# Hybrid decoder trunk, one core: the recurrent layer's sum x and its product with the input gate formed on VectorE instead of GpSimd, three small state copies moved the other way, and all state rows in one tile with one load and one store

## The chip, the cores and the metric

The kernel runs on one core of a Trainium2 chip. Times are device microseconds (us) of one execution of the whole program; several executions give a median. A separate execution is recorded by the hardware profiler. Its span is counted from its first to its last recorded instruction, and its own time is a little longer than the span. In the rows of the profile PE is TensorE's matmuls, PEld its weight loads, DVE is VectorE, ACT is ScalarE, POOL is GpSimd and SP is SyncE, which here only issues DMAs.

## What is computed

The reference runs two layers over 1024 prompt positions and 8 further one-token sequences, in float32. Layer 0 mixes tokens with a gated linear recurrence, layer 1 with sliding-window attention; a squared-ReLU MLP follows each. The change touches layer 0's mixer alone:

```python
def recurrent_block(x, h0, conv_prev, w_in, conv_w, conv_b, w_a, b_a, w_x, b_x, lam, w_out):
    u = x @ w_in
    gate, xr = jnp.split(u, 2, axis=-1)
    xc, conv_new = causal_conv(xr, conv_prev, conv_w, conv_b)
    y, h_new = rg_lru(xc, h0, w_a, b_a, w_x, b_x, lam)
    return (y * jax.nn.gelu(gate)) @ w_out, h_new, conv_new
```

`rg_lru` forms two gates r and i as sigmoids of small products of xc, a decay a = exp(-8 r softplus(-lam)), an input u = sqrt(1 - a²) (i xc), and scans h = a h + u along the positions. Besides its output the layer returns the new states: the last h of the prompt and of each of the 8 sequences, and the last three inputs of the convolution for each of them.

## The kernel before

Features lie on partitions and the 1032 tokens on the free axis, so the width of 1024 is eight tiles of 128x1032, m = 0 to 7; a matmul takes a third of the tokens (344). Full precision comes from splitting each operand in a high and a low part, `hi` (a cast on ACT, lines 165 and 253) and `lo` (a subtraction on DVE, lines 166 and 254), and from three matmuls per product (line 226).

Layer 0's mixer is a list of stages, `LRU` (line 55): c1 c0 x4 g0 c2 c3 r0 c4 x5 g1 c5 r1 x7 x6 g2 r2 c7 o5 c6 o0 o1 o3 g3 r3 o6 o2 o4 o7, after `xr_first`, which computes x for m = 0 to 3. The stages are these:

- x (`xr_stage`, `conv_evac`): the projection; DVE takes each third out of PSUM (line 1129, at high priority) and POOL starts the convolution from it (line 1130).
- c (`conv`): three taps on DVE for the prompt (line 1135), two small copies that keep the last columns, into `cst` (line 1136) and `cvp` (line 1137), three small operations for the 8 sequences that read `cst` (line 1139), then the split into `xch` and `xcl`.
- g (`gates`): for a pair of tiles (2 kb, 2 kb + 1) four products, whose PSUM banks ACT empties with sigmoids at high priority (line 1163). The results are `ri`.
- r (`recur`): for each tile of the pair t = xch + xcl on POOL (line 1172) and i = i t on POOL (line 1173). Then ACT overwrites t with a tanh (line 1175), so it waits for line 1173; then exp (line 1177) and squares (line 1182) on ACT, line 1183 on DVE, a square root on ACT (line 1185), and on DVE the product (line 1188), the scan (line 1189), two operations of 8 columns for the sequences (lines 1190 and 1191) and a copy of the last states into `hno` (line 1192).
- o (`gate_out`): the gate's projection, emptied by DVE (line 1201), GeLU on ACT (line 1202), the product with t in place on DVE (line 1203), and the split for the layer's last product.

Each engine has one queue and takes its instructions in order. That order isn't the order of the program text: a scheduler fills the queues by its own estimate of when each instruction is ready, by priority, where earlier text means higher priority. A wait at the head of a queue therefore holds all behind it. Tiles of 128x1032 come from a pool of 33 (`A`) and one of 12 (`W`); a stage starts only when a slot is free. Weights are fetched by SP (line 159) into a few raw buffers, ahead of their split. One split of a weight in the recurrent layer, that of unit 13, is done by POOL (line 166) and not by DVE.

The states lie in four tiles: `cst` (the old three inputs of each sequence and the new one), `h0`, `cvp` and `hno`. `cst` and `h0` are loaded by two DMAs on SP (lines 1093 and 1095); three DMAs on SP store the new states after stage r3 (lines 1213 to 1215).

Of the kernel before, what the change touches and what calls it, by code (L numbers as in the profile page):

```python
# [10 lines left out]
F32 = mybir.dt.float32  # L11
F32R = mybir.dt.float32r
AF = mybir.ActivationFunctionType
ALU = mybir.AluOpType
PSUM = bass.MemoryType.PSUM

P = 128
D = 1024
M8 = D // P
SEQ = 1024  # L20
NS = 8
T = SEQ + NS
CH = T // 3
NCH = 3
DFF = 4096
NB = SEQ // P
HALF = T // 2
CHUNKS = [range(0, 3), range(3, 6), range(6, 9), range(9, 12), range(12, 14)]
NSP = CHUNKS[-1][-1] + 1
RQ = 2 * P * max(len(c) for c in CHUNKS)  # L30
QT = T // 4
NPAIR = DFF // (2 * P)
# [27 lines left out]
def trunk(ctx: ExitStack, tc: tile.TileContext, I, O):  # L60
    nc = tc.nc
    pe, act, dve, pool, sp = nc.tensor, nc.scalar, nc.vector, nc.gpsimd, nc.sync

    cp = ctx.enter_context(tc.tile_pool(name="cp", bufs=1))
# [24 lines left out]
    def nm(s):  # L89
        cnt[0] += 1  # L90
        return f"{s}{cnt[0]}"

    def A(s="a"):
        return ap.tile([P, T], F32, tag="A", name=nm(s))

    def W(s="w"):
        return wp.tile([P, T], F32, tag="W", name=nm(s))

    def S(s="s"):
        return small["pool"].tile([P, CH], F32, tag="S", name=nm(s))  # L100

    BANKS = {"N": 1, "P": 3, "S": 2, "T": 1, "O": 1}
    ring = ["P", "P", "P", "S", "S", "T"]
    turn = [0]

    def B(tag=None):
        if tag is None:
            tag = ring[turn[0] % len(ring)]
            turn[0] += 1
        return psum["pool"].tile([P, 512], F32, tag=tag, bufs=BANKS[tag], name=nm("b" + tag))  # L110
# [14 lines left out]
    def cs(c):  # L125
        return slice(c * CH, (c + 1) * CH)
# [12 lines left out]
    def V(n, m=0):  # L139
        o, _ = VEC[n]  # L140
        return vec[:, o + m:o + m + 1]
# [34 lines left out]
    for o in [("x", m) for m in range(4)] + LRU:  # L176
        if o[0] == "g":
            units.append(("gate", o[1], I["w_gate"][o[1]], W))
        elif o[0] in "xo":
            m = o[1] + (8 if o[0] == "x" else 0)  # L180
# [71 lines left out]
    def split_act_dve(hi, lo, src, sl, eng=dve):  # L252
        act.copy(r_(hi[:, sl]), src)
        eng.tensor_tensor(r_(lo[:, sl]), src, hi[:, sl], ALU.subtract)
# [437 lines left out]
    def attention(hs):  # L692
# [9 lines left out]
        qrow = aux[:, 0:P]  # L702
        qblk = qrow.rearrange("p (n t u i) -> p n t u i", n=NS, t=2, u=2)
        pool.memset(qrow, 0.0)
        ks = aux[:, P:P + 2 * NS].rearrange("p (t n) -> p t n", t=2)
        den = [cp.tile([P, 4], F32, name=f"den{i}") for i in range(4)]
# [82 lines left out]
        def v_proj():  # L789
# [22 lines left out]
            ps = B("T")  # L812
            mms(ps[:NS, :256], slice(SEQ, T))
            vo = S("vo")
            act.copy(vo[:NS, :256], ps[:NS, :256])
            sp.dma_start(vnew.rearrange("h (n j) -> (h n) j", n=4), vo[:NS, :256])

# [271 lines left out]
            ensure(3)  # L1089

    sp.dma_start(con, I["con"])
    cst = cp.tile([P, M8, 4, NS], F32, name="cst")
    sp.dma_start(cst[:, :, 0:3, :], I["conv_state"])
    h0 = cp.tile([P, M8, NS], F32, name="h0")
    sp.dma_start(h0, I["h_state"])
    cvp = cp.tile([P, M8, 3], F32, name="cvp")
    hno = cp.tile([P, M8, 1 + NS], F32, name="hno")


    sp8 = cp.tile([P, M8], F32, name="sp8")  # L1100
    lam = nsp8 = VV("lam")
# [18 lines left out]
    ys = {}  # L1120
# [11 lines left out]
    def conv(m):  # L1132
        xr, xc = xrc.pop(m)
        for d, w in ((1, "cw2"), (2, "cw1"), (3, "cw0")):
            dve.scalar_tensor_tensor(xc[:, d:SEQ], xr[:, 0:SEQ - d], V(w, m), xc[:, d:SEQ], ALU.mult, ALU.add)  # L1135
        dve.tensor_copy(cst[:, m, 3, :], xr[:, SEQ:T])
        dve.tensor_copy(cvp[:, m, :], xr[:, SEQ - 3:SEQ])
        for k, w in ((2, "cw2"), (1, "cw1"), (0, "cw0")):
            dve.scalar_tensor_tensor(xc[:, SEQ:T], cst[:, m, k, :], V(w, m), xc[:, SEQ:T], ALU.mult, ALU.add)
        hi, lo = A("xch"), A("xcl")  # L1140
        split_act_dve(hi, lo, xc, slice(0, T))
        xcs[m] = (hi, lo)
# [23 lines left out]
    def recur(kb):  # L1166
        ms = (2 * kb, 2 * kb + 1)
        for m in ms:
            i = rr[m, 1]
            xh, xl = xcs.pop(m)  # L1170
            ys[m] = (W if m in (2, 3, 5, 7) else A)("t")
            pool.tensor_tensor(ys[m], xh, xl, ALU.add)  # L1172
            pool.tensor_tensor(i, i, ys[m], ALU.mult)  # L1173
        for m in ms:
            act.activation(ys[m], rr[m, 0], AF.Tanh, scale=sp8[:, m:m + 1])
        for m in ms:
            act.activation(rr[m, 0], rr[m, 0], AF.Exp, scale=nsp8[:, m:m + 1])
        for m in ms:
            r, t = rr[m, 0], ys[m]
            for c in range(NCH):  # L1180
                a2 = S("a2")
                act.activation(a2, r[:, cs(c)], AF.Square)
                dve.scalar_tensor_tensor(t[:, cs(c)], a2, 1.0, t[:, cs(c)], ALU.add, ALU.mult)
        for m in ms:
            act.activation(ys[m], ys[m], AF.Sqrt)
        for m in ms:
            r, i, t = rr.pop((m, 0)), rr.pop((m, 1)), ys[m]
            dve.tensor_tensor(i, t, i, ALU.mult)
            dve.tensor_tensor_scan(t[:, :SEQ], r[:, :SEQ], i[:, :SEQ], 0.0, ALU.mult, ALU.add)
            dve.tensor_tensor(t[:, SEQ:T], r[:, SEQ:T], h0[:, m, :], ALU.mult)  # L1190
            dve.tensor_tensor(t[:, SEQ:T], t[:, SEQ:T], i[:, SEQ:T], ALU.add)
            dve.tensor_copy(hno[:, m, :], t[:, SEQ - 1:T])

    gos = {}

# [14 lines left out]
    for what, i in LRU:  # L1210
        stages[what](i)
        if (what, i) == ("r", 3):
            sp.dma_start(O["conv"][:, :, 3:27].rearrange("p m (k n) -> p m k n", k=3), cst[:, :, 1:4, :])
            sp.dma_start(O["conv"][:, :, 0:3], cvp)
            sp.dma_start(O["h"], hno)
    gl = [gos[m] for m in range(M8)]
    pin_tables()
    spill, spill0, spill1 = [tc.dram_tile([M8, P, T], F32, name=f"spill{i}") for i in range(3)]
# [31 lines left out]

_OUT_SHAPES = {
    "y": (M8, P, T),
    "conv": (P, M8, 27),
    "h": (P, M8, 9),
    "k": (2, P, P),
    "v": (P, 256),
    "ks": (2, P, D),
# [41 lines left out]
def _layout(a):  # L1299
    f = lambda n: np.asarray(a[n])  # L1300
    out = {}
    x = np.concatenate([f("x_prompt")[0], f("x_sample")[:, 0]], 0)
    out["xT"] = x.T.reshape(M8, P, T)
    out["w_in"] = _mtiles(f("lru_w_in")[0])
    out["w_gate"] = np.stack([f("lru_w_a")[0], f("lru_w_x")[0]], 1).reshape(4, 2, 2, P, 256).transpose(0, 3, 2, 1, 4).reshape(4, P, D)
    out["w_out0"] = _mtiles(f("lru_w_out")[0])
    out["w_up"] = np.stack([_pair_blocks(f("mlp_w_up")[l]) for l in range(2)])
    out["w_dn"] = np.stack([_down_units(f("mlp_w_down")[l]) for l in range(2)])
    perm = np.concatenate([np.arange(h * 64, h * 64 + 64) for h in HEAD_PERM])
    wqkv = f("attn_w_qkv")[0]  # L1310
    wv = wqkv[:, 1280:1536].reshape(2, 4, P, 256).transpose(0, 2, 1, 3).reshape(2, P, D)
    out["w_qkv"] = np.concatenate([_mtiles(wqkv[:, perm]), _mtiles(wqkv[:, 1024:1280]), wv])
    out["w_out1"] = _mtiles(f("attn_w_out")[0][perm])
    vec = np.zeros((P, NVEC), np.float32)

    def put(n, v):
        o, w = VEC[n]
        vec[:, o:o + w] = v

    cols = lambda v: v.reshape(M8, P).T  # L1320
    put("g_mix0", cols(f("norm_mix_g")[0]))
    put("g_mix1", cols(f("norm_mix_g")[1]))
    put("g_mlp0", cols(f("norm_mlp_g")[0]))
    put("g_mlp1", cols(f("norm_mlp_g")[1]))
    for k in range(4):
        put(f"cw{k}", cols(f("lru_conv_w")[0, k]))
    put("cb", cols(f("lru_conv_b")[0]))
    put("ba", cols(f("lru_b_a")[0]))
    put("bx", cols(f("lru_b_x")[0]))
    put("lam", cols(f("lru_lambda")[0]))  # L1330
    put("qg", np.tile(f("attn_q_norm")[0], 2)[:, None])
    put("kg", np.tile(f("attn_k_norm")[0], 2)[:, None])
    sinks = f("attn_sinks")[0]
    put("sinks", np.broadcast_to(sinks, (P, 16)))
    heads = np.array([(2 * p + u) * 4 + i for n in range(NS) for p in range(2) for u in range(2) for i in range(4)])
    put("sink_row", sinks[heads][:, None])
    put("slope_row", np.array([-SLOPES[h] for h in heads], np.float32)[:, None])
    put("eps", np.float32(EPS))
    out["vec"] = vec
    out["con"], out["dist_s"] = _constants()  # L1340
    out["conv_state"] = f("state_rglru_conv")[0].reshape(NS, 3, M8, P).transpose(3, 2, 1, 0)
    out["h_state"] = f("state_rglru_h")[0].reshape(NS, M8, P).transpose(2, 1, 0)
    kc = f("cache_swa_k")[0][:, 1:]
    out["k_cache"] = kc.reshape(NS, 127, 2, P).transpose(2, 3, 0, 1)
    out["v_cache"] = f("cache_swa_v")[0][:, 1:].reshape(NS, 127, 256).transpose(1, 0, 2)
    return {k: np.ascontiguousarray(v) for k, v in out.items()}
# [34 lines left out]
```

## Time and profile before

| what | us |
|---|---|
| median of 3 executions | 2031.12 (2030.24 to 2034.45) |
| profiled execution, its own time | 2033.93 |
| its span | 2032.2 |
| busy in the span: PE, DVE, ACT, POOL | 2001.2, 1413.9, 1056.3, 352.8 |

The recurrent layer takes the first 260 us or so of the span, and its list of stages begins at about 50 us. Attention and the two MLPs take the rest. Of the views used below, the windows give the busy time of each engine in stretches of the span with the granted TensorE clock (PEclk, where 1.00 is full speed); the waits give for each engine what it sat idle for; the timeline gives the instructions in order, neighbours of one kind merged, as start, duration, engine, line, operation, output and inputs.

### The profile page before, as it was taken

What the parts mean: (1) busy time and instruction counts of PE and PEld (TensorE: products, weight loads), DVE (VectorE), ACT (ScalarE), POOL (GpSimd) and SP (SyncE); (2) the same over time, 40 slices, a digit from 0 to 9 for tenths busy, and PEclk for the clock granted to TensorE, in tenths of its full rate; (3) what the DMA queues carried; (4) which work ended last, traced back from release to release, by engine and by line L of the source; (5) the groups of instructions that cost most, each with busy time, mean ns of one, the idle gap of its engine ahead of it and who ended that gap; (6) DMA issues with size and microseconds to landing.
All of it is one profiled execution on the core that took longest, in us unless ns stands there. A gap on an engine that the chain in (4) does not pass through costs nothing.

```text
span 2032.2 us, 38742 instructions
## 1 busy us (share of the span) xinstructions
PE 2001.2 (98%) x15106; PEld 1956.2 (96%) x15106; DVE 1413.9 (70%) x2673; ACT 1056.3 (52%) x2090; POOL 352.8 (17%) x562
## 2 busy tenths in 40 slices
PE   8989999999999999999999999999999999999999
PEld 8979999999999999999988887899999999999999
DVE  7887637876766867666846677569776767766663
ACT  6475635543343655555457777546434346555550
POOL 2541100000000333321003444100000003332220
PEclk9989999999999999999999999999999999999999
DMA  5102142244344787877443435712534446887783
GB/s 176 52 32 55 53 164 87 99 152 152 136 152 162 245 231 206 229 197 178 130 109 84 107 94 168 247 59 70 189 138 150 142 166 226 228 217 212 203 199 105
DMA packets 121047, 304.87 MB, mean 150 GB/s; under 512 B 20888, under 2 KB 53152, under 8 KB 120864
## 3 DMA queue, kind: packets, MB, share of 16 engines
q1 hardware_dynamic: 64864, 135.41, 22.1%
q0 software_dynamic: 28352, 98.30, 19.0%
q10 hardware_dynamic: 27648, 68.70, 9.2%
q8 instruction: 118, 1.93, 0.4%
q14 instruction: 65, 0.53, 0.1%
HBM read 176.22 MB, written 113.44 MB: 143 GB/s over the span
## 4 chain that ended last, share of the span: by engine, by line
PE 89%; DVE 2%; ACT 2%; issue 1%; POOL 1%; DMA 1%; SPq 0%; ACTq 0%; POOLq 0%
PE bD L529 60%; PE bP L226 11%; PE bS L226 6%; PE bP L771 4%; PE bT L226 3%; PE bO L892 1%; PE bS L851 1%; PE bT L871 1%; PE bN L717 1%; POOL t L1172 1%; PE bS L799 1%; POOL ri L1173 0%; DVE wl L166 0%; DVE xc L1135 0%; DMA od0l<-o 0%
## 5 line engine op out<-in xcount | busy, mean ns | idle before, releaser
L529 PE MATMUL bD<-op,op 128*128 128x258 f32 x5376 | 648.5, 283 | 0.0
L529 PEld LDWEIGHTS bD<-op,op 128*128 128x128 f32 x5376 | 647.9, 190 | 0.4
L529 PE MATMUL bD<-tl,op 128*128 128x258 f32 x4704 | 567.7, 283 | 0.0
L529 PEld LDWEIGHTS bD<-tl,op 128*128 128x128 f32 x4704 | 566.7, 190 | 0.8 <-DVE ho L640 0.2
L542 POOL DMA_DIRECT2D tl<-hsum x196 | 116.1, 712 | 913.1 <-DMA hsum<-he 420.8
L396 DVE TENSOR_TENSOR op<-ws,op 128x512 fp32r<-128x512 f32 (+2 forms) x288 | 170.6, 598 | 80.0 <-ACT op L395 80.0
L402 DVE TENSOR_TENSOR tl<-tl 128x516 fp32r<-128x516 f32 x196 | 130.9, 694 | 122.7 <-ACT tl L401 122.6
L636 ACT COPY ho<-bD 128x516 f32<-128x516 f32 x144 | 85.1, 591 | 244.1 <-PE bD L529 241.7
L395 ACT CAST op<-ws 128x512 fp32r<-128x512 f32 (+2 forms) x288 | 155.8, 550 | 56.2 <-DVE op L396 27.1
L396 DVE TENSOR_TENSOR op<-raw,op 128x512 fp32r<-128x512 f32 (+2 forms) x216 | 124.5, 597 | 57.8 <-ACT op L395 57.8
L636 ACT COPY he<-bD 128x516 f32<-128x516 f32 x144 | 84.0, 583 | 134.6 <-PE bD L529 125.3
L395 ACT CAST op<-raw 128x512 fp32r<-128x512 f32 (+2 forms) x216 | 114.5, 549 | 34.9 <-PE bD L529 22.7
L401 ACT CAST tl<-tl 128x516 fp32r<-128x516 f32 x196 | 114.9, 627 | 2.8 <-DMA tl<-hsum 2.8
L649 ACT ACTIVATE ho<-ho 128x1032 f32<-128x1032 f32 x32 | 34.2, 1070 | 107.3 <-DVE ho L648 107.3
L166 DVE TENSOR_TENSOR wl<-raw,wh 128x1024 fp32r<-128x1024 f32 (+1 forms) x57 | 68.2, 1202 | 25.5 <-ACT wh L165 20.6
L862 POOL TENSOR_SCALAR se<-se,den 128x256 f32<-128x256 f32 (+1 forms) x128 | 66.1, 521 | 77.2 <-DVE den L860 75.3
L165 ACT CAST wh<-raw 128x1024 fp32r<-128x1024 f32 (+1 forms) x60 | 58.6, 988 | 37.7 <-DMA raw<-w_in 15.9
L855 DVE CUSTOM_DVE_ANT_0 se<-bS,bias,nsink 128x256 f32<-128x256 f32 (+1 forms) x128 | 56.4, 461 | 21.6 <-PE bS L851 16.8
L655 POOL DMA_DIRECT2D spill<-ho x32 | 28.7, 896 | 242.2 <-DVE ho L644 232.6
L858 ACT ACTIVATE se<-se,den 128x257 f32<-128x257 f32 (+1 forms) x128 | 63.0, 496 | 14.7 <-DVE den L855 13.0
L644 DVE TENSOR_TENSOR ho<-bD,ho 128x516 f32<-128x516 f32 x72 | 49.8, 692 | 23.0 <-PE bD L529 23.0
L640 DVE TENSOR_TENSOR ho<-bD,ho 128x516 f32<-128x516 f32 x72 | 49.7, 690 | 16.0 <-PE bD L529 9.1
(299 smaller groups left out, 3745.5 us busy)
## 6 DMA issues: line engine op xcount, KB each, us to landing
tl<-hsum POOLq DMA_DIRECT2D x196, 258.0 KB, 7.8
raw<-w_up SPq DMA_DIRECT2D x64, 512.0 KB, 3.7
raw<-w_dn SPq DMA_DIRECT2D x64, 384.0 KB, 5.6
spill<-ho POOLq DMA_DIRECT2D x32, 516.0 KB, 6.7
spill<-he POOLq DMA_DIRECT2D x32, 516.0 KB, 7.9
hsum<-ho ACTq DMA_DIRECT2D x28, 516.0 KB, 3.7
hsum<-he ACTq DMA_DIRECT2D x28, 516.0 KB, 2.7
hsum<-ts ACTq DMA_DIRECT2D x28, 516.0 KB, 3.4
```

The costliest lines, as they stand in the source:

```text
L166: eng.tensor_tensor(r_(lo[:, sl]), raw[:, sl], hi[:, sl], ALU.subtract)
L226: pe.matmul(o, lhsT=r_(wt[:, col(k):col(k) + P]), rhs=r_(xt[:, cs(c)]), start=(k == first and a == 0), stop=(k == final and a == 2))
L395: act.copy(r_(t[:, 0:n]), src)
L396: dve.tensor_tensor(r_(t[:, n:2 * n]), src, t[:, 0:n], ALU.subtract)
L401: act.copy(r_(hi), lo)
L402: dve.tensor_tensor(r_(lo), lo, hi, ALU.subtract)
L529: pe.matmul(d[:, 512 * b:512 * b + QT], lhsT=r_(wt[:, j * P:j * P + P]), rhs=r_(xt[:, QT * b:QT * b + QT]), start=first and j == 0 and a = ...
L542: pool.dma_start(t[:, n:2 * n], src)
L636: last["copy"] = act.copy(t, f).ins
L771: pe.matmul(ps[c], lhsT=r_(wt[:, k * P:k * P + P]), rhs=r_(xt[:, cs(c)]), start=(k == 0 and a == 0), stop=(k == M8 - 1 and a == 2))
L858: act.activation(se[:, u, 256 - n:257], se[:, u, 256 - n:257], AF.Exp, scale=-1.0, bias=dn[:, u:u + 1], accum_out=dn[:, 2 + u:3 + u])
L862: pool.tensor_scalar(e, e, dn[:, 2 + u:3 + u], 0.0, ALU.mult, ALU.add)
```

## The change

1. Lines 1172 and 1173, eight instructions each on 128x1032, go from POOL to DVE.
2. The copies of lines 1136, 1137 and 1192, eight each on 128x8, 128x3 and 128x9, go from DVE to POOL.
3. The four state tiles become one, `st`, of 52 columns per m. One DMA loads it, with the host leaving gaps where results will be written, and one DMA stores all of it after stage r3. The host cuts the results out.

```diff
-    cst = cp.tile([P, M8, 4, NS], F32, name="cst")
-    sp.dma_start(cst[:, :, 0:3, :], I["conv_state"])
-    h0 = cp.tile([P, M8, NS], F32, name="h0")
-    sp.dma_start(h0, I["h_state"])
-    cvp = cp.tile([P, M8, 3], F32, name="cvp")
-    hno = cp.tile([P, M8, 1 + NS], F32, name="hno")
-
+    st = cp.tile([P, M8, NST], F32, name="st")
+    sp.dma_start(st, I["states"])
+    h0, hno, cvp = st[:, :, 35:43], st[:, :, 43:52], st[:, :, 32:35]
+
+    def cst(m, k):
+        return st[:, m, k * NS:(k + 1) * NS]
...
-        dve.tensor_copy(cst[:, m, 3, :], xr[:, SEQ:T])
-        dve.tensor_copy(cvp[:, m, :], xr[:, SEQ - 3:SEQ])
+        pool.tensor_copy(cst(m, 3), xr[:, SEQ:T])
+        pool.tensor_copy(cvp[:, m, :], xr[:, SEQ - 3:SEQ])
         for k, w in ((2, "cw2"), (1, "cw1"), (0, "cw0")):
-            dve.scalar_tensor_tensor(xc[:, SEQ:T], cst[:, m, k, :], V(w, m), xc[:, SEQ:T], ALU.mult, ALU.add)
+            dve.scalar_tensor_tensor(xc[:, SEQ:T], cst(m, k), V(w, m), xc[:, SEQ:T], ALU.mult, ALU.add)
...
-            pool.tensor_tensor(ys[m], xh, xl, ALU.add)
-            pool.tensor_tensor(i, i, ys[m], ALU.mult)
+            dve.tensor_tensor(ys[m], xh, xl, ALU.add)
+            dve.tensor_tensor(i, i, ys[m], ALU.mult)
...
-            dve.tensor_copy(hno[:, m, :], t[:, SEQ - 1:T])
+            pool.tensor_copy(hno[:, m, :], t[:, SEQ - 1:T])
...
-            sp.dma_start(O["conv"][:, :, 3:27].rearrange("p m (k n) -> p m k n", k=3), cst[:, :, 1:4, :])
-            sp.dma_start(O["conv"][:, :, 0:3], cvp)
-            sp.dma_start(O["h"], hno)
+            sp.dma_start(O["states"], st)
```

More of the change, by code (lines that the diff above doesn't have):

```diff
@@ L21 @@
 NS = 8
+NST = 52
 T = SEQ + NS
@@ L1252 @@
     "y": (M8, P, T),
-    "conv": (P, M8, 27),
-    "h": (P, M8, 9),
+    "states": (P, M8, NST),
     "k": (2, P, P),
@@ L1340, in _layout @@
     out["con"], out["dist_s"] = _constants()
-    out["conv_state"] = f("state_rglru_conv")[0].reshape(NS, 3, M8, P).transpose(3, 2, 1, 0)
-    out["h_state"] = f("state_rglru_h")[0].reshape(NS, M8, P).transpose(2, 1, 0)
+    conv = f("state_rglru_conv")[0].reshape(NS, 3, M8, P).transpose(3, 2, 1, 0).reshape(P, M8, 24)
+    h = f("state_rglru_h")[0].reshape(NS, M8, P).transpose(2, 1, 0)
+    gap = lambda n: np.zeros((P, M8, n), np.float32)
+    out["states"] = np.concatenate([conv, gap(11), h, gap(9)], 2)
     kc = f("cache_swa_k")[0][:, 1:]
@@ L1369 @@
     ys = y[SEQ:].reshape(NS, 1, D)
-    h = o["h"].transpose(2, 1, 0).reshape(9, D)
+    st = o["states"].transpose(2, 1, 0).reshape(NST, D)
+    h = st[43:]
     hp = h[0].reshape(1, 1, D)
     hsm = h[1:].reshape(1, NS, D)
-    cv = o["conv"].transpose(2, 1, 0).reshape(27, D)
-    cvp = cv[:3].reshape(1, 1, 3, D)
-    cvs = cv[3:].reshape(3, NS, D).transpose(1, 0, 2).reshape(1, NS, 3, D)
+    cvp = st[32:35].reshape(1, 1, 3, D)
+    cvs = st[8:32].reshape(3, NS, D).transpose(1, 0, 2).reshape(1, NS, 3, D)
     kp = o["k"].reshape(256, P).T.reshape(1, 1, P, 4, 64)
```

## The prediction

> **What bounds the kernel now.** I read the page first, for which engine sets the end.
>
> ```profile
> PE 2001.2 (98%) x15106; PEld 1956.2 (96%) x15106; DVE 1413.9 (70%) x2673; ACT 1056.3 (52%) x2090; POOL 352.8 (17%) x562
> ...
> PE 89%; DVE 2%; ACT 2%; issue 1%; POOL 1%; DMA 1%; SPq 0%; ACTq 0%; POOLq 0%
> ```
>
> PE is busy 98% of the span and carries 89% of the chain. The change removes no matmul, so it can win only where PE stands still or runs at a lowered clock inside the recurrent layer. PE's waits in the first 420 us, then windows cut at its gaps (stretch, length, then busy us of PE, PEld, DVE, ACT, POOL with counts, PEclk), show where that is.
>
> ```profile
> PE bP L226 <- ACT ri L1163: 6.3, 3, 5.0
> PE bS L226 <- DVE xr L1129: 3.9, 1, 3.9
> ```
>
> ```profile
> 101.12:106.09 4.97, 0.01 (x2) 0.00 (x1) 3.41 (x7) 4.94 (x10) 4.58 (x4) 0.72 0.00 0
> 106.09:111.20 5.11, 5.07 (x19) 4.49 (x19) 5.11 (x10) 5.05 (x7) 0.00 (x0) 0.61 0.02 3
> 111.20:114.52 3.32, 2.61 (x15) 2.33 (x15) 2.51 (x4) 2.30 (x6) 0.00 (x0) 1.00 0.00 0
> ...
> 140.77:144.62 3.85, 0.00 (x0) 0.00 (x0) 3.85 (x6) 1.14 (x3) 0.00 (x0) 0.95 0.00 0
> 144.62:151.08 6.46, 6.46 (x22) 6.18 (x22) 6.44 (x11) 2.24 (x4) 6.40 (x5) 0.50 0.47 162
> ```
>
> There are two real stalls. **Stall 1**: 4.97 us idle for ACT's sigmoids of g1, then 5.11 us at a clock of 0.61, which costs another 5.11 x 0.39 = 2.0. **Stall 2**: 3.85 us idle for DVE to empty x6's banks, then 6.46 us at 0.50, another 3.2. Together they cost 14.0 us. The third row holds 3.32 - 2.61 = 0.7 us of idle time and keeps 1.00.
>
> **Why PE stalls.** ACT's order behind stall 1, and POOL's:
>
> ```profile
> ACT t L1175 <- POOL ri L1173: 15.1, 5, 6.7
> POOL ri L1173 <- ACT ri L1163: 12.5, 3, 9.4
> ```
>
> ```profile
> 46.20 0.63 POOL L1130 TENSOR_SCALAR xc<-xr,vec 128x344 f32<-128x344 f32 x1 [3.72 <-DVE xr L1129]
> ...
> 82.21 3.37 POOL L1172 TENSOR_TENSOR t<-xch,xcl 128x1032 f32<-128x1032 f32 x1 [4.36 <-ACT ri L1163]
> 88.10 3.34 POOL L1172 TENSOR_TENSOR t<-xch,xcl 128x1032 f32<-128x1032 f32 x1 [2.52 <-DVE xcl L254]
> 91.40 5.78 POOL L1173 TENSOR_TENSOR ri<-ri,t 128x1032 f32<-128x1032 f32 x2
> ...
> 119.72 3.80 POOL L1173 TENSOR_TENSOR ri<-ri,t 128x1032 f32<-128x1032 f32 x1 [2.25 <-ACT ri L1163]
> ...
> 137.59 3.06 POOL L166 TENSOR_TENSOR wl<-raw,wh 128x1024 fp32r<-128x1024 f32 x1 [8.74 <-ACT wh L165]
> ```
>
> ```profile
> 97.22 1.16 ACT L1175 ACTIVATE t<-ri,sp 128x1032 f32<-128x1032 f32 x1 [1.23 <-POOL ri L1173]
> ...
> 105.49 1.43 ACT L1163 ACTIVATE ri<-bP,vec 128x344 f32<-128x344 f32 x3
> ...
> 119.04 0.55 ACT L1163 ACTIVATE ri<-bT,vec 128x344 f32<-128x344 f32 x1
> ```
>
> POOL ends r0's second product at 91.40 + 5.78 = 97.18. The second tanh starts at 97.22, and from there to the sigmoid at 105.49 ACT is busy with r0's exponentials, squares and table loads. So POOL's end sets stall 1, one for one: 8.3 us later the bank comes free, and PE resumes at 106.09.
>
> **The same work on DVE.** Two lines' instructions, durations in ns (min/median/max):
>
> ```profile
> L1188 DVE TENSOR_TENSOR ri<-t,ri x8: 1225/1230/1235, 109.7 to 232.9; 128x1032 f32<-128x1032 f32 x8
> ```
>
> ```profile
> L1136 DVE COPY cst<-xr x8: 157/163/172, 50.3 to 161.4; 128x8 f32<-128x8 f32 x8
> ```
>
> Line 1188 is the same operation on the same shape, so each moved instruction takes 1.23 us instead of the 2.9 (half of 5.78) to 3.8 of the rows above; sixteen add 19.7 us to DVE. What DVE loses is seen in its timeline:
>
> ```profile
> 83.17 2.44 DVE L1139 SCALAR_TENSOR_TENSOR xc<-cst,vec,xc 128x8 f32<-128x8 f32 x1
> 85.53 1.21 DVE L166 TENSOR_TENSOR wl<-raw,wh 128x1024 fp32r<-128x1024 f32 x1
> 86.66 0.22 DVE L1139 SCALAR_TENSOR_TENSOR xc<-cst,vec,xc 128x8 f32<-128x8 f32 x1
> 86.80 5.73 DVE L254 TENSOR_TENSOR xcl<-xc,xch 128x1032 fp32r<-128x1032 f32 x3
> ...
> 119.03 2.29 DVE L1189 TENSOR_TENSOR_SCAN t<-ri,ri 128x1024 f32<-128x1024 f32 x1
> 121.24 2.32 DVE L1190 TENSOR_TENSOR t<-ri,h 128x8 f32<-128x8 f32 x1
> ...
> 138.38 2.29 DVE L1190 TENSOR_TENSOR t<-ri,h 128x8 f32<-128x8 f32 x1
> ...
> 142.85 0.15 DVE L1190 TENSOR_TENSOR t<-ri,h 128x8 f32<-128x8 f32 x1
> 142.93 1.21 DVE L166 TENSOR_TENSOR wl<-raw,wh 128x1024 fp32r<-128x1024 f32 x1
> 144.07 0.93 DVE L1129 TENSOR_TENSOR xr<-bS,rt 128x344 f32<-128x344 f32 x2
> ```
>
> An 8-column operation with two inputs takes 0.15 to 0.22 us, but 2.3 to 2.4 us when POOL's long sum or product runs beside it (83.17 beside 82.21, 121.24 beside 119.72): the two exclude each other. At 138.38 it is POOL's weight split, which stays.
>
> *Stall 1.* DVE's three splits end at 86.80 + 5.73 = 92.53. Without POOL beside them, 83.17 loses 2.2 and the splits lose 5.73 - 3 x 1.23 = 2.0; r0's four moved instructions add 4.9. Even if the last product comes last, it ends at 92.53 - 4.2 + 4.9 = 93.2, instead of 97.18. The copies of c0 to c4 (ten) come before: 0.4 us, below. That makes 93.6, a gain of 3.6: PE would idle 1.4 instead of 4.97.
>
> *Stall 2.* r1's last product starts on POOL when the last sigmoid is there (119.04 + 0.55) and ends at 123.52. On DVE it meets the scan of 119.03: ahead of it the product ends at 120.8, behind it at 122.6; I take the middle, 1.8 earlier than now. The scans behind it, and with them the emptying at 144.07, follow. Idle goes from 3.85 to 2.0. r1's other three instructions cost DVE 3.7; its wait of 2.2 at 121.24 goes, and the rest falls in idle time of 3.98 us before line 1188 at 117.76:
>
> ```profile
> 117.76 1.23 DVE L1188 TENSOR_TENSOR ri<-t,ri 128x1032 f32<-128x1032 f32 x1 [3.98 <-ACT t L1185]
> ```
>
> *The clock.* After 0.7 us of idle it stayed at 1.00, after 3.85 it was 0.50. Idle times of 1.4 and 2.0 lie between; both are nearer to 0.7, so I let the slow stretches go (2.0 and 3.2). If they stay, the sum is 5.4 instead of 10.6.
> The Trainium skill ("TensorE: Matmul & The Clock Gate", section "Why this matters for your kernels") bids one leave no PE gap above about 3 us between bursts, else the clock falls to half. The trace agrees at both ends (0.7 us at 1.00, 3.85 us at 0.50), and by that rule the sum is 10.6.
>
> *The copies on POOL.* The trace has no small copy on POOL. Bounds: 0, and 0.63 us, POOL's 344-column operation at 46.20 alone. The DVE copy of the same shape takes 0.16; I take 0.2, being nearer to it in size, so ten cost DVE at most 10 x 0.04 = 0.4 if each holds DVE up for its whole time.
> Against this change speaks the Trainium skill, "SBUF — State Buffer", section "SBUF: two separate sides": VectorE and GpSimd share a port pair as an exclusive lock, held for a whole instruction. The trace agrees (0.15 against 2.3 us); by it every copy on POOL can stop DVE, at its full length. [...]
>
> *Waits added.* Line 1203 writes over t in place, so its last third waits for POOL's copy into the states; on DVE weight splits and PSUM emptying (lines 166, 1201) queue behind it. At 0.2 us, eight times, I cost it at nothing: PE runs without a gap there, on six banks. Without that cover it is up to 8 x 0.63 = 5.0.
>
> ```profile
> 178.00:203.00 25.00, 25.00 (x161) 25.00 (x160) 18.22 (x32) 9.73 (x14) 1.66 (x1) 1.00 0.27 86
> ```
>
> *DMAs.* The load is read first at 53.5 us, long after its issue:
>
> ```profile
> L1139 DVE SCALAR_TENSOR_TENSOR xc<-cst,vec,xc x24: 211/220/2435, 53.5 to 162.1; 128x8 f32<-128x8 f32 x24
> ...
> L1093 SPq DMA_DIRECT2D cst<-conv_state x1: 654/654/654, 19.9 to 19.9; - x1
> ```
>
> ```profile
> SPq L1215 <- DVE hno L1192: 21.8, 1, 21.8
> SPq L1213 <- DVE xc L1139: 17.1, 1, 17.1
> ```
>
> Of SP's two waits for stores the second stays, now for POOL's last copy, with the w_out loads behind it as today; the first, with w_in loads behind, goes. PE has no wait for weights there, so neither counts. The rows of the one tile are disjoint. Were the tile ordered as a whole, c5's reads would come after r0's last copy, behind 121.24 + 2.32 = 123.6, with some 4 us to its split; PE takes x5 only in g2, which starts 3 us ahead of the gap at 140.77. Hidden by some 10 us.
>
> **Sum.** Stall 1: 3.6 + 2.0; stall 2: 1.8 + 3.2; together 10.6. The profiled execution took 2033.93, so 2023.3 for its like; it lay 2.8 above the median of 2031.12, from which I predict 2020.5.
>
> **Rivals.**
>
> - *Half of it* (2025.7): the clock falls after the shorter gaps too, or stall 2 stays as DVE's order puts the scans ahead of x6's emptying (142.93, then 144.07, as now). 5.4 to 5.6 us. For it: that order comes from estimates made before the run. Against: both chains start earlier.
> - *Given back* (2031.1): a moved product waits for its sigmoid at the head of DVE's queue. POOL waited 12.5 us so in three places, at no cost. On DVE 3.98 us of idle time cover part of the 9.4; the remaining 5.4 stand against the scan and x6's emptying and eat the gain of stall 1 (5.6), while stall 2 stays.
> - *Slower* (2036): the copies on POOL hold DVE up. At x us each the last product of r0 ends at 93.2 + 10 (x - 0.16); from x = 0.56 on stall 1 isn't shorter. At 0.63 it is 0.7 longer, six copies of c5, r0 and r1 lengthen stall 2 by 6 x 0.47 = 2.8, and of the 5.0 us of waits before line 1203 a third, 1.7, comes through to PE, whose six banks cover the rest: 5.2 in all, or 8.5 with all 5.0. For it: DVE is the fuller engine. Against: POOL's time for 8 columns should lie well below that for 344.
> - *Nothing done*: both moves are explicit engine names, so the instructions move; no chance of its own.
>
> **How the numbers follow.** Chances: forecast 0.41, half 0.20, given back 0.17, slower 0.22. A measurement can tell about 0.2% (4 us) from no change: faster 0.61, same 0.17, slower 0.22. Lower end: both stalls with their slow stretches gone (14.0), the small gap as well (0.7), and 0.9 for the spread of the runs below their median (2030.24): 2015.5. Upper end: 2037, with the likelier half of the slower case. Left out are some 0.02 below and 0.1 above. The forecast alone spans 2015.5 to 2024.
>
> **What would show it.** Right: lines 1172 and 1173 on DVE at 1.23 us; no 2.3 us operation of 8 columns in r0 to r2 save beside line 166; the second tanh of r0 about 94, the sigmoid of g1 about 102; PEclk at 1.00 from 76 to 152; POOL's copies near 0.2. Wrong: a PE wait for `xr` or `ri` of over 3 us, a DVE wait for ACT's `ri` of some us before line 1173, or copies of 0.5 us and more. Were PE 10 us early and the total unchanged, the time would have gone to a new wait after 150 us.

## The result and the profile after

The changed kernel takes 2017.72 us, the median of 6 executions (2017.08 to 2019.35), against 2031.48 for the kernel before beside it (6 executions, 2030.24 to 2034.45). The ratio is 0.9932, with a 95% interval of 0.9919 to 0.9944: faster by 0.68%, or 13.8 us. The profiled execution took 2018.72 us, its span is 2016.9; before it was 2033.93 and 2032.2.

The page of the kernel after, its busy times and its chain:

```profile
PE 1995.5 (99%) x15106; PEld 1951.8 (97%) x15106; DVE 1411.6 (70%) x2665; ACT 1054.7 (52%) x2089; POOL 321.9 (16%) x570
...
PE 92%; DVE 4%; ACT 2%; issue 1%; DMA 1%; POOL 0%; SPq 0%; ACTq 0%; DVEq 0%
```

The matmuls are the same 15106. DVE, which took over sixteen instructions of 128x1032, isn't busier than before (1413.9): the 19.7 us of the new work are set off by the copies that left and by the eight-column operations and splits that POOL's long instructions no longer hold up. POOL lost 30.9 us. What the change won must then be time in which PE stood still or ran slowly. Windows over the part of the recurrent layer around both stalls, before and then after (stretch, length, busy us and instructions of PE, PEld, DVE, ACT and POOL, granted clock, DMA share, GB/s):

```profile
76.00:203.00 127.00, 117.42 (x710) 115.58 (x709) 100.96 (x134) 80.02 (x110) 50.24 (x25) 0.95 0.16 43
```

```profile
76.00:203.00 127.00, 125.78 (x793) 124.48 (x792) 105.20 (x138) 88.62 (x126) 20.07 (x26) 1.00 0.15 47
```

In the same 127 us PE now does 793 matmuls instead of 710, at a clock of 1.00 instead of 0.95. A matmul takes 0.155 us at full clock (161 in a stretch of 25.00 us without a gap, in the first row below), so 83 of them are 12.9 us. The two profiled executions differ by 15.2 us, and the medians by 13.8: most of the gain comes from this stretch. The two windows that held the stalls, in the kernel after:

```profile
102.00:127.00 25.00, 25.00 (x161) 25.00 (x161) 22.41 (x32) 24.84 (x35) 3.36 (x7) 1.00 0.04 9
127.00:152.00 25.00, 24.43 (x151) 23.54 (x150) 23.98 (x28) 13.84 (x20) 10.98 (x8) 1.00 0.26 78
```

PE has no gap at all in the first and 0.57 us in the second. The waits of PE in the first 420 us, where before stood 6.3 us for ACT's `ri` (one of 5.0) and 3.9 for DVE's `xr`, say the same; `xr` isn't on the list any more, and the longest wait for `ri` is 0.7 (total, times, longest):

```profile
PE bP L227 <- ACT ri L1163: 1.2, 2, 0.7
```

How stall 1 went: DVE's timeline around r0, and ACT's (start, duration, engine, line, operation, in brackets the idle time before and what ended it).

```profile
88.23 2.37 DVE L1172 TENSOR_TENSOR t<-xch,xcl 128x1032 f32<-128x1032 f32 x2
90.52 2.37 DVE L1173 TENSOR_TENSOR ri<-ri,t 128x1032 f32<-128x1032 f32 x2
```

```profile
91.84 2.24 ACT L1175 ACTIVATE t<-ri,sp 128x1032 f32<-128x1032 f32 x2 [2.38 <-DVE ri L1173]
...
97.51 0.47 ACT L1182 ACTIVATE a<-ri 128x344 f32<-128x344 f32 x1
...
99.29 1.43 ACT L1163 ACTIVATE ri<-bP,vec 128x344 f32<-128x344 f32 x3
```

r0's last product ends at 90.52 + 2.37 = 92.89 instead of 97.18, and g1's first sigmoid starts at 99.29 instead of 105.49: 4.3 us of that is the product, the rest is ACT's order. Only one of r0's six squares (line 1182) stands ahead of the sigmoids; the others follow later.

How stall 2 went: the first of r1's scans on DVE before, and DVE's timeline around both scans after.

```profile
136.18 2.28 DVE L1189 TENSOR_TENSOR_SCAN t<-ri,ri 128x1024 f32<-128x1024 f32 x1
```

```profile
128.43 2.27 DVE L1189 TENSOR_TENSOR_SCAN t<-ri,ri 128x1024 f32<-128x1024 f32 x1
130.63 0.90 DVE L1129 TENSOR_TENSOR xr<-bS,rt 128x344 f32<-128x344 f32 x2
...
131.95 2.27 DVE L1189 TENSOR_TENSOR_SCAN t<-ri,ri 128x1024 f32<-128x1024 f32 x1
```

x6's emptying (line 1129) starts at 130.63, between r1's two scans. Before, it stood behind both scans and a weight split, at 144.07. Of these 13.4 us, 7.8 are those by which the first scan itself starts earlier; the other 5.7 are the order, since DVE's queue now has the emptying behind one scan only.

### The profile page after: what moved, and what is told of

Same layout as the page of the kernel before. It is cut to its first block, busy times and chain, and to the rows that moved or that the text cites. A ratio compares the mean times of both kernels' runs of the same rounds, so it can differ in the third digit from the quotient of the medians.

```text
span 2016.9 us, 38731 instructions
## 1 busy us (share of the span) xinstructions
PE 1995.5 (99%) x15106; PEld 1951.8 (97%) x15106; DVE 1411.6 (70%) x2665; ACT 1054.7 (52%) x2089; POOL 321.9 (16%) x570
## 4 chain that ended last, share of the span: by engine, by line
PE 92%; DVE 4%; ACT 2%; issue 1%; DMA 1%; POOL 0%; SPq 0%; ACTq 0%; DVEq 0%
PE bD L530 60%; PE bP L227 12%; PE bS L227 6%; PE bP L772 4%; PE bT L227 3%; PE bS L852 1%; PE bO L893 1%; PE bT L872 1%; PE bN L718 1%; DVE sq L278 1%; PE bS L800 1%; DVE wl L167 0%; DMA raw<-w_in 0%; ACT wh L166 0%; DVE t L1189 0%
## 5 line engine op out<-in xcount | busy, mean ns | idle before, releaser
L166 ACT CAST wh<-raw 128x1024 fp32r<-128x1024 f32 (+1 forms) x60 | 58.7, 988 | 38.8 <-DMA raw<-w_in 12.9
L645 DVE TENSOR_TENSOR ho<-bD,ho 128x516 f32<-128x516 f32 x72 | 49.7, 690 | 22.9 <-PE bD L530 22.9
L273 ACT ACTIVATE sq<-y 128x344 f32<-128x344 f32 x48 | 23.6, 492 | 71.4 <-DVE y L363 60.8
```

## The theories

Three explanations of the 13.8 us had to be told apart; each expectation below says in its own words what it makes of its run.

- *Length*: POOL's sums and products took 2.4 to 3.8 us each where DVE takes 1.23. r0's last product ended late, and with it ACT's sigmoids; the rest followed from that.
- *Exclusion*: POOL's long instructions held up DVE's, so that it is their presence beside DVE's work that counted, whichever of them moves.
- *States*: the copies on POOL, the one tile and the fewer DMAs bring some of the time.

A further question came up with the trace of after: whether stall 2 went because DVE had less to do, or because the queue's order changed, and what changed it.

## The experiments

Ratios are to the kernel before, run on the same chip, with 95% intervals. The gaps and clocks are those of one profiled execution each; starts differ by about 1 us between executions, so gaps are compared and not absolute times. Line numbers are those of each run's own kernel: the weight split of line 166 is line 167 in the kernel after and all that come from it, and an edit shifts the lines behind it.

### The moves alone: e1_moves_only

The kernel before, with nothing but lines 1172 and 1173 changed.

```diff
-            pool.tensor_tensor(ys[m], xh, xl, ALU.add)
-            pool.tensor_tensor(i, i, ys[m], ALU.mult)
+            dve.tensor_tensor(ys[m], xh, xl, ALU.add)
+            dve.tensor_tensor(i, i, ys[m], ALU.mult)
```

> The kernel before with only lines 1172 and 1173 on VectorE; copies, tiles and DMAs as before. Theory 1 (the early end of the product frees ACT, so PE's banks come free in time) and theory 2 (VectorE is no longer held up by GpSimd's long instructions) both expect all of the gain: 2016 to 2020 us, no PE wait over 1 us in the recurrent layer. Theory 3 (the copies off VectorE, the one tile or SP's missing wait matter) expects at least a third of the 14 us to be missing: 2022 us or more.

Measured: 0.9938 (0.9921 to 0.9954). In the profiled execution both stalls are gone, and x6's emptying stands between r1's scans as in after. That execution was the fastest of four, 2016.45 us; the other three took 2020.90 to 2021.90. So the two moved lines bring the whole gain as far as can be told: a part of 1 or 2 us for the states, the copies on POOL and the DMAs isn't excluded, but they are not the cause of the gain.

### The states alone: e2_states_only

The kernel after, with both lines back on POOL.

```diff
-            dve.tensor_tensor(ys[m], xh, xl, ALU.add)
-            dve.tensor_tensor(i, i, ys[m], ALU.mult)
+            pool.tensor_tensor(ys[m], xh, xl, ALU.add)
+            pool.tensor_tensor(i, i, ys[m], ALU.mult)
```

> The kernel after with the sum and the product back on GpSimd; copies on GpSimd and one tile as after. Theories 1 and 2 expect no gain: 2029 to 2034 us, both PE stalls there. Theory 3 expects 2026 us or less.

Measured: 0.9983 (0.9974 to 0.9992), 3.5 us by the ratio and 2.7 by the medians; 2030.34 us lies where theories 1 and 2 put it. Stall 1 stays, but stall 2 is shorter, which neither expected. PE's waits, and POOL's timeline:

```profile
PE bP L227 <- ACT ri L1163: 6.0, 3, 4.8
...
PE bS L227 <- DVE xr L1129: 2.1, 2, 1.7
```

```profile
140.08 1.13 POOL L1192 COPY st<-t 128x9 f32<-128x9 f32 x1 [11.22 <-DVE t L1190]
141.18 2.37 POOL L167 TENSOR_TENSOR wl<-raw,wh 128x1024 fp32r<-128x1024 f32 x1
```

A copy into the states, moved to POOL, waits there for r1's eight-column operations on DVE (line 1190), and POOL's weight split is queued behind it. The split therefore no longer runs beside r1's scan chain, as it did at 137.59 before, where it held an eight-column operation on DVE for 2.29 us. So the copies do something on their own, by way of POOL's queue; with the moves in place e1_moves_only and after don't show anything of it, stall 2 being gone then.

### The sum alone: e3_sum_only

The kernel after, with the product (line 1173) back on POOL.

```diff
-            dve.tensor_tensor(i, i, ys[m], ALU.mult)
+            pool.tensor_tensor(i, i, ys[m], ALU.mult)
```

> The kernel after with the product (line 1173) back on GpSimd, the sum on VectorE. Theory 1: r0's two products take 2 x 2.4 us on GpSimd after the sums, so the last ends at about 95.4 instead of 97.2 before and 92.9 after; stall 1 keeps some 3 us and stall 2 stays, 2025 to 2030 us. Theory 2: half of the long GpSimd instructions are gone, half of the gain, 2023 to 2026 us.

Measured: 0.9957 (0.994 to 0.9973), 2024.61 us: in the range of theory 2 and just below that of theory 1. Around stall 1 PE has gaps of 1.04, 1.81 and 0.71 us, and the clock stays at 1.00 behind them. At r1 the gaps are 0.88 and 0.42 us, so stall 2 didn't stay, as theory 1 had it, though x6's emptying is behind both scans and the split again. POOL does r0's two products in a row, beside DVE's work:

```profile
88.43 6.64 POOL L1173 TENSOR_TENSOR ri<-ri,t 128x1032 f32<-128x1032 f32 x2 [11.81 <-ACT xch L254]
```

```profile
89.35 3.45 DVE L255 TENSOR_TENSOR xcl<-xc,xch 128x1032 fp32r<-128x1032 f32 x1
92.72 4.58 DVE L1172 TENSOR_TENSOR t<-xch,xcl 128x1032 f32<-128x1032 f32 x2
```

The products end at 95.07, between the 92.89 of after and the 97.18 of before (by more than the 1 us of the starts), and the gaps lie between as well. That is the order that the length of the chain through r0 would give, but length isn't alone here: a split takes 3.45 us instead of 1.23 and two sums 4.58 instead of 2.37. The gap of 1.04 is a wait for DVE, which empties x5's banks only behind them, at 97.23.

### The product alone: e4_product_only

The kernel after, with the sum (line 1172) back on POOL.

```diff
-            dve.tensor_tensor(ys[m], xh, xl, ALU.add)
+            pool.tensor_tensor(ys[m], xh, xl, ALU.add)
```

> The kernel after with the sum (line 1172) back on GpSimd, the product on VectorE. Theory 1: the sums are ready before the last sigmoid but for r0's second one, so only the product's length counts; r0's last product ends at about 92 to 94, nearly all of the gain, 2017 to 2021 us. Theory 2: half of the long GpSimd instructions are gone, half of the gain, 2023 to 2026 us.

Measured: 0.9994 (0.9985 to 1.0004), no gain that can be told from none; neither expectation had that. At stall 1 the gaps are 1.30 and 2.34 us; behind the second the clock fell. Stall 2 became longer than before. PE's longest wait and the rows of DVE and POOL ahead of it:

```profile
PE bS L227 <- DVE xr L1129: 6.7, 2, 5.4
```

```profile
129.68 4.57 DVE L1188 TENSOR_TENSOR ri<-t,ri 128x1032 f32<-128x1032 f32 x2
134.18 4.52 DVE L1189 TENSOR_TENSOR_SCAN t<-ri,ri 128x1024 f32<-128x1024 f32 x1
```

```profile
130.36 2.80 POOL L167 TENSOR_TENSOR wl<-raw,wh 128x1024 fp32r<-128x1024 f32 x1 [1.75 <-ACT wh L166]
...
134.14 2.41 POOL L1172 TENSOR_TENSOR t<-xch,xcl 128x1032 f32<-128x1032 f32 x1 [0.98 <-PE bT L227]
```

The two products of line 1188 take 4.57 us beside POOL's split, against 2.36 in after, and the scan takes 4.52 beside POOL's sum, against 2.27. x6's emptying stands behind both scans again, at 142.21. So one moved line wins nothing when the other meets DVE's chain at a worse place: exclusion is real, but it is priced by where the two meet.

### After again, for the same chip: e5_after_again

The kernel after unchanged, as the base for the runs beside it.

> The kernel after once more, as the measure for the three runs beside it on this chip: 0.9932 of the kernel before, as first measured, within 0.1%.

Measured: 0.9936 (0.9923 to 0.995), median 2018.71 us, with the same gaps.

### Only r0 back on POOL: e6_r0_pool

The kernel after, with the sum and the product of r0, four instructions of sixteen, on POOL.

```diff
-            dve.tensor_tensor(ys[m], xh, xl, ALU.add)
-            dve.tensor_tensor(i, i, ys[m], ALU.mult)
+            (pool if kb == 0 else dve).tensor_tensor(ys[m], xh, xl, ALU.add)
+            (pool if kb == 0 else dve).tensor_tensor(i, i, ys[m], ALU.mult)
```

> The kernel after with the sum and the product of r0 alone back on GpSimd; r1 to r3 on VectorE. New theory (two stalls with two causes: the late product in r0 makes stall 1; GpSimd's long instructions beside r1's scans, and the place of x6's emptying in VectorE's queue, make stall 2): stall 1 comes back with its slow clock, 7 us, stall 2 at most in part; 2024 to 2027 us. Rival (r0's delay alone makes both): both stalls, 2029 us or more.

Measured: 0.9987 (0.9978 to 0.9996). The four instructions take back most of the gain. POOL's products, then DVE's queue at stall 2:

```profile
89.77 6.78 POOL L1173 TENSOR_TENSOR ri<-ri,t 128x1032 f32<-128x1032 f32 x2
```

```profile
134.49 2.28 DVE L1189 TENSOR_TENSOR_SCAN t<-ri,ri 128x1024 f32<-128x1024 f32 x1
...
136.75 2.28 DVE L1189 TENSOR_TENSOR_SCAN t<-ri,ri 128x1024 f32<-128x1024 f32 x1
...
139.08 1.21 DVE L167 TENSOR_TENSOR wl<-raw,wh 128x1024 fp32r<-128x1024 f32 x1
140.22 0.50 DVE L1129 TENSOR_TENSOR xr<-bS,rt 128x344 f32<-128x344 f32 x1
```

r0's last product ends at 96.55 (the profile starts about 1 us earlier than that of before), PE idles 1.14 and 3.71 us and then runs at a lowered clock: stall 1 is back. r1 has both operations on DVE as in after, and yet x6's emptying is behind both scans and the split again. The gaps there are 1.04 and 0.42 us, at a clock of 1.00. So neither expectation holds whole: 2030.46 us is the rival's time, but stall 2 is back only in small part. What four instructions of r0 decide is stall 1 and, with nothing changed at r1, the order of DVE's queue there; e9_squares_first shows by what way.

### x6's emptying behind the scans: e7_empty_behind

The kernel after with one thing more, an order within DVE's own queue, which needs no semaphore (`NoSync`): x6's emptying comes after r1's second scan. No work is added. `last` only keeps an instruction by name, here the later scan of each pair.

```diff
-            dve.tensor_tensor(xr[:, cs(c)], o, rx[:, cs(c)], ALU.mult)
+            e = dve.tensor_tensor(xr[:, cs(c)], o, rx[:, cs(c)], ALU.mult)
+            if m == 6:
+                tc.add_manual_dep(e.ins, last['scan', 1].name, mybir.DependencyInfo(mybir.DependencyClass.NoSync, mybir.DependencyReason.DATA), reason='order')
...
-            dve.tensor_tensor_scan(t[:, :SEQ], r[:, :SEQ], i[:, :SEQ], 0.0, ALU.mult, ALU.add)
+            last['scan', kb] = dve.tensor_tensor_scan(t[:, :SEQ], r[:, :SEQ], i[:, :SEQ], 0.0, ALU.mult, ALU.add).ins
```

> The kernel after with an edge that only orders VectorE's queue: x6's emptying (line 1129) goes behind r1's second scan instead of between the two. Nothing is computed differently. If the queue's order at this place matters: the emptying starts 2.3 us later, at 132.9, PE idles 1.7 us, and the time rises by 1.7 us if the clock holds, by 3 to 5 if it falls. Rival (the order is of no weight, only the early products count): no PE wait there, no change.

Measured: 0.995 (0.9938 to 0.9963), median 2022.43, 3.7 us more than the kernel after beside it. The two intervals overlap; that a gap opened is seen in the trace. PE's timeline, and a window from the gap on:

```profile
132.16 0.85 PE L227 MATMUL bS<-xch,wh 128*128 128x344 f32 x2 [1.60 <-DVE xr L1129]
```

```profile
131.00:136.00 5.00, 3.84 (x15) 3.37 (x16) 4.91 (x10) 1.64 (x3) 3.69 (x3) 0.79 0.17 26
```

One scan of 2.28 us ahead of the emptying opens a gap of 1.60 us, and the clock falls behind it. From 76 to 203 us PE does 778 matmuls, and in the run of after beside it 792:

```profile
76.00:203.00 127.00, 124.74 (x778) 123.57 (x777) 103.00 (x136) 88.52 (x126) 16.70 (x25) 0.99 0.16 46
```

14 x 0.155 = 2.2 us are lost there, by the medians 3.7. So the place of three short instructions in one queue costs some 2 to 4 us of the 13.8, and part of that is the clock, which other runs below show to hold behind gaps as long.

### The squares ahead of the sigmoids: e9_squares_first

The kernel after, with g1's first three sigmoids ordered behind all six squares of r0 in ACT's queue.

```diff
-                        act.activation(o[:, cs(c)], ps[c], AF.Sigmoid, bias=V(b, 2 * kb + mm))
+                        e = act.activation(o[:, cs(c)], ps[c], AF.Sigmoid, bias=V(b, 2 * kb + mm))
+                        if (kb, mm, g) == (1, 0, 0):
+                            tc.add_manual_dep(e.ins, last['sqr', 0].name, mybir.DependencyInfo(mybir.DependencyClass.NoSync, mybir.DependencyReason.DATA), reason='order')
...
-                act.activation(a2, r[:, cs(c)], AF.Square)
+                last['sqr', kb] = act.activation(a2, r[:, cs(c)], AF.Square).ins
```

> The kernel after with an edge that only orders ScalarE's queue: g1's first three sigmoids go behind all six squares of r0, as in the kernel before, instead of behind the first square. If the early product alone removes stall 1: the sigmoid starts about 101.2 instead of 99.3, PE idles about 1 us at most, and the time rises by 0 to 1.5 us. If the new order of ScalarE's queue does the work: 4 us or more.

Measured: 0.9941 (0.9928 to 0.9953), 1.5 us more than after in the medians, which the intervals don't resolve. ACT's and PE's timelines:

```profile
96.53 2.37 ACT L1184 ACTIVATE a<-ri 128x344 f32<-128x344 f32 x6
...
100.22 0.55 ACT L1163 ACTIVATE ri<-bP,vec 128x344 f32<-128x344 f32 x1
```

```profile
100.81 0.43 PE L227 MATMUL bP<-xch,wh 128*128 128x344 f32 x1 [1.06 <-ACT ri L1163]
```

PE idles 1.06 us, about what the prediction had left at stall 1 (1.4), and the clock holds. So ACT's new order, with most of the squares later, is what took the rest of that stall.

The edge names ACT alone, and yet DVE's queue at r1 has the order of before again:

```profile
129.80 2.28 DVE L1191 TENSOR_TENSOR_SCAN t<-ri,ri 128x1024 f32<-128x1024 f32 x1
...
132.13 1.21 DVE L167 TENSOR_TENSOR wl<-raw,wh 128x1024 fp32r<-128x1024 f32 x1
133.27 0.50 DVE L1129 TENSOR_TENSOR xr<-bS,rt 128x344 f32<-128x344 f32 x1
```

x6's emptying is behind both scans and the split, with gaps of 0.88 and 0.42 us and a clock of 1.00. So this run has both old orders, and what it takes over after, 1.5 us as far as they are real, is the price of both. It also shows what the order at r1 hangs on. In before, e2_states_only, e3_sum_only, e4_product_only, e6_r0_pool and here, four or six of r0's squares stand ahead of g1's sigmoids, and the emptying is behind both scans; in after, e1_moves_only, e8_split_dve and e10_r0_vector_only one square does, and it is between them. Where the scheduler puts g1's sigmoids thus goes with what it does in DVE's queue 30 us later.

### The last long POOL instruction: e8_split_dve

The kernel after, with unit 13's split on DVE as well. It takes away the one place left around the stalls where POOL holds DVE for over 2 us. (Unit 3's split is on POOL too and stays there; in the trace of before it runs at 21 us, ahead of the list of stages.) In the kernel after, the tap on DVE beside POOL's split, which takes 2.37 us from 139.93 on:

```profile
139.97 3.40 DVE L1135 SCALAR_TENSOR_TENSOR xc<-xr,vec,xc 128x1022 f32<-128x1022 f32 x1
```

```diff
-                loaded[(n, j)] = split_unit(raws[nloaded[0]], alloc, pool if nloaded[0] in (3, 13) else dve,
+                loaded[(n, j)] = split_unit(raws[nloaded[0]], alloc, pool if nloaded[0] in (3,) else dve,
```

> The kernel after with the weight split of unit 13 on VectorE, the last long GpSimd instruction beside stage c6. It adds 1.2 us to VectorE and takes away the 2.1 us for which line 1135 is held at 139.97. PE waits nowhere for that, so all theories expect the time of the kernel after within 1 us (0.993 to 0.994 of the kernel before); 0.9925 or less would say that GpSimd still costs PE time there.

Measured: 0.9934 (0.9922 to 0.9947), the same as after, although that tap now takes 1.27 us. With PE's gaps closed, a hold on DVE that PE doesn't wait for is worth nothing that can be measured here.

### Only r0 on VectorE: e10_r0_vector_only

The kernel after, with r1 to r3 back on POOL, the reverse of e6_r0_pool.

```diff
-            dve.tensor_tensor(ys[m], xh, xl, ALU.add)
-            dve.tensor_tensor(i, i, ys[m], ALU.mult)
+            (pool if kb > 0 else dve).tensor_tensor(ys[m], xh, xl, ALU.add)
+            (pool if kb > 0 else dve).tensor_tensor(i, i, ys[m], ALU.mult)
```

> The kernel after with the sum and the product of r1, r2 and r3 back on GpSimd, r0 alone on VectorE. If r0's late product is the root of both stalls: nearly all of the gain, 2017 to 2022 us, no stall 1 and x6's emptying between the two scans as after. If GpSimd's long instructions beside r1 are what makes stall 2: stall 2 comes back with its slow clock, 2023 to 2027 us.

Measured: 0.9953 (0.9939 to 0.9966), median 2024.66 us, a time that the second expectation gave. But stall 2 is gone, with x6's emptying between the scans again, as the first had it. Stall 1 is partly back, with gaps of 1.10 and 1.75 us and a lowered clock, which wasn't in either expectation. (The profiled execution is the slowest of the five; the last section says why.) POOL's and DVE's timelines:

```profile
86.12 6.69 POOL L1172 TENSOR_TENSOR t<-xch,xcl 128x1032 f32<-128x1032 f32 x2 [9.59 <-DVE xcl L255]
```

```profile
87.03 6.88 DVE L1172 TENSOR_TENSOR t<-xch,xcl 128x1032 f32<-128x1032 f32 x2
93.83 2.36 DVE L1173 TENSOR_TENSOR ri<-ri,t 128x1032 f32<-128x1032 f32 x2
```

POOL forms r1's sums while DVE forms r0's. DVE is held, its two sums take 6.88 us instead of the 2.37 of after, and r0's last product ends at 96.19 although it is on DVE: here exclusion alone makes the chain late, by 4.5 us. Length and exclusion are thus two ways to the same delay. The end is about as late as in e6_r0_pool (96.55), and yet the order at r1 is that of after: the order was fixed by estimates made before the run, not by when the product ended in it.

### The queue order alone, in the kernel before: e11_before_empty_first

The kernel before, with both lines on POOL, and only an order on DVE's queue: r1's second scan, its products with `h0`, one weight split and c7's later taps come behind x6's emptying. (The lines that keep these instructions in `last` are left out.)

```diff
+            if m == 6:
+                last['x6'] = e.ins
+                for late in (last['scan', 3], last['h0', 2], last['h0', 3], last['wl', 12]):
+                    tc.add_manual_dep(late, e.ins.name, mybir.DependencyInfo(mybir.DependencyClass.NoSync, mybir.DependencyReason.DATA), reason='order')
...
+            if m == 7 and d > 1:
+                tc.add_manual_dep(e.ins, last['x6'].name, mybir.DependencyInfo(mybir.DependencyClass.NoSync, mybir.DependencyReason.DATA), reason='order')
```

> The kernel before with edges that only order VectorE's queue: x6's emptying goes ahead of r1's second scan, of the two 8-column products, of a weight split and of c7's second tap. Sum and product stay on GpSimd. If stall 2 is a matter of that place in the queue: stall 1 stays (4.97 us and 2.0 of slow clock), stall 2 goes with its slow clock, 7 us less, 2023 to 2027 us. If the emptying is late because r1's products are: stall 2 stays over 2 us, 2028 us or more.

Measured: 0.9964 (0.9951 to 0.9976), 7.3 us by the ratio and 5.1 by the medians (2032.59 and 2027.45, 0.45 above the expected range). PE's longest waits, and the two windows:

```profile
PE bP L226 <- ACT ri L1169: 5.7, 3, 4.9
```

```profile
102.00:127.00 25.00, 22.36 (x122) 21.64 (x123) 18.41 (x26) 21.95 (x28) 9.95 (x7) 0.86 0.00 1
127.00:152.00 25.00, 24.79 (x156) 24.27 (x156) 24.62 (x29) 16.17 (x26) 13.98 (x8) 1.00 0.23 65
```

Stall 1 is as before (a wait of 4.9 us for `ri`, clock 0.86), and stall 2 is gone, with no instruction moved between engines. Its price was 3.85 idle and 3.2 at the lowered clock, 7.05 together: what came back agrees with that within the interval.

No version tried is faster than the kernel after.

## Why the prediction was right in direction and short in size

It gave 2020.5 us, faster; measured were 2017.72, 2.8 lower and within the range.

- **What bounds the kernel** was read rightly: two stalls of PE with a slow stretch behind each, 14.0 us in all by the trace of before. 13.8 came back, and e11_before_empty_first gives stall 2's part by itself (5.1 to 7.3 us).
- **Stall 1's cause** was right: POOL's end of r0's last product. It was forecast to end on DVE at 93.2, or 93.6 with the copies, and did at 92.89; the second tanh, forecast about 94, began near 93 (two in 2.24 us from 91.84), and the sigmoid, forecast about 102, at 99.29. The near hit of the product is luck in part: the sum had all three splits ahead of it, while one of 1.23 us went behind, and DVE waited 1.94 us for ACT's cast, which the sum hadn't.
- **The mis-sized terms** are the idle times that were to remain. "PE would idle 1.4 instead of 4.97" and "idle goes from 3.85 to 2.0" came out as none at both places. These 3.4 us are about the distance between the sum of 10.6 and the measured 13.8. Both steps carried the old order of a queue forward, ACT's tail of 8.3 us behind the tanh and DVE's scans ahead of x6's emptying, and moved it as a block. The scheduler wrote both orders anew once r0's sum and product stood on DVE. With both old orders back, as in e9_squares_first, gaps of 1.06 us and of 0.88 and 0.42 us appear and the median is 2020.18 us, close to the forecast; the 1.5 us above after are not resolved, so the order as the whole of the difference is likely and not shown. The prediction had named the order only as a risk (the rival of half the gain), and not as a thing that could turn out better.
- **The clock step** was right by luck. It let the clock hold behind 1.4 and 2.0 us, as nearer to 0.7 than to 3.85. Behind gaps of that size it held in some runs (1.70 us in e2_states_only, 1.81 in e3_sum_only) and fell in others (1.60 in e7_empty_behind, 1.75 in e10_r0_vector_only). That did no harm only because no such gap was left.
- **Durations on DVE** were right: 1.22 to 1.23 us per moved instruction, and no eight-column operation of 2.3 us any more (durations in ns, min/median/max):

```profile
L1190 DVE TENSOR_TENSOR t<-ri,st x8: 140/144/447, 111.1 to 220.5; 128x8 f32<-128x8 f32 x8
```

- **The copies on POOL**, the *slower* rival, take what was estimated when they run alone, and more beside some of DVE's work (two of POOL's rows, DVE's row beside the first of them, and all eight copies of line 1192 in ns):

```profile
50.74 1.25 POOL L1136 COPY st<-xr 128x8 f32<-128x8 f32 x1
...
77.41 0.19 POOL L1136 COPY st<-xr 128x8 f32<-128x8 f32 x1
```

```profile
50.73 1.21 DVE L167 TENSOR_TENSOR wl<-raw,wh 128x1024 fp32r<-128x1024 f32 x1
```

```profile
L1192 POOL COPY st<-t x8: 191/773/1912, 111.6 to 221.3; 128x9 f32<-128x9 f32 x8
```

So copies of over 0.5 us, which the prediction had among the signs of being wrong, did come, and cost nothing that can be seen. That rival assumed that a copy of x us holds DVE for x us. The long one shown is a copy that waits for DVE, for the whole split, while DVE keeps its 1.21 us. The Trainium skill ("SBUF — State Buffer", section "SBUF: two separate sides") has one lock that either engine can lose, for a whole instruction; these rows and the 4.52 us scan agree with it.

- **The rival "given back"** needed a product at the head of DVE's queue waiting for its sigmoid. DVE sat idle before none of the eight products of line 1173.
- **The DMAs and the one tile** were costed at nothing: e1_moves_only and after can't be told apart.

## What to carry to other kernels

When a busy engine waits on a chain through other engines, price the end of that chain and the clock's slow stretch behind the gap, not the busy time that a move saves: DVE's total hardly changed here, and 0.68% came from a product that ended 4.3 us earlier and from the queue orders that came with it. A moved instruction can make the scheduler order other queues anew, so the order of before is no basis for what is left of a stall. Look for the short instruction that empties a bank: its place behind one more scan cost 2.2 to 3.7 us, and putting it ahead gained 5.1 to 7.3 us in the old kernel without moving any work.

## What the hardware showed beside that

The granted clock doesn't go by the length of the idle gap alone. Two runs have nearly the same two gaps at the same place, 1.04 and 1.81 us in e3_sum_only, 1.10 and 1.75 us in e10_r0_vector_only. A stretch of 3 us, some 3 us behind the second gap, in each:

```profile
106.00:109.00 3.00, 3.00 (x21) 3.00 (x20) 3.00 (x4) 2.95 (x4) 2.99 (x1) 1.00 0.00 0
```

```profile
106.00:109.00 3.00, 3.00 (x13) 3.00 (x13) 3.00 (x3) 2.13 (x6) 1.87 (x1) 0.58 0.00 0
```

PE does 21 matmuls at 1.00 in the first and 13 at 0.58 in the second. The clock also held behind 1.70 us in e2_states_only; it fell behind 2.34 us in e4_product_only (0.66 over 3 us) and behind the 1.60 of e7_empty_behind. The rule of about 3 us in the Trainium skill ("TensorE: Matmul & The Clock Gate", section "Why this matters for your kernels"), with which the prediction's two rows agreed, isn't borne out below it: three shorter gaps were followed by a lowered clock.

It can fall with no gap ahead of it, too. In the second layer, which no version changes, the profiled execution of e10_r0_vector_only has these two stretches in a row:

```profile
1312.00:1327.00 15.00, 14.93 (x104) 14.38 (x102) 7.19 (x17) 6.86 (x15) 0.00 (x0) 1.00 0.10 36
1327.00:1337.00 10.00, 10.00 (x42) 10.00 (x41) 2.10 (x6) 1.67 (x4) 0.00 (x0) 0.50 0.05 18
```

PE is busy 14.93 of 15 us, and then works 10 us at half the clock, with 42 matmuls where the rate of the row above gives 69: some 4 us lost. That execution was the slowest of its five, 2029.56 us against 2023.65 to 2025.58. The profiled executions of after and e5_after_again show no such stretch. So some us of the difference between two executions can come from a place that the change doesn't touch, and a clock that fell behind a short gap in one profiled execution is no price of that gap. What decides stays open.
